# Mixer products in float32r of split weights, with projections in groups of 512 columns

## The chip, the cores and the metric

The kernel runs on one core of one Trainium2 chip. The metric is device time in microseconds (us) of one launch. Inputs, outputs and the reference's arithmetic are float32.

## The reference, cut to what matters

The network has two layers, a sequence of 256 positions and a width of 1024. Each layer first mixes tokens, then runs a mixture of experts (16 experts of width 256). The token mixer is where the change lies:

```
h = modulate(rms_norm(x, g_mix[l]), sh1, sc1)
proj = h @ w_in                      # 256x1024 by 1024x2340
cu, cg, dq, dk, dv, iq, ik, iw, mq, mk, mv = jnp.split(proj, offs, axis=-1)
y_conv = conformer_conv(cu, cg, ...) # gate, 31 taps per channel, layer norm, silu
y_dsa  = dsa_attention(dq, dk, dv, iq, ik, iw)   # 6 heads, each query keeps its top 64 keys
y_moba = moba_attention(mq, mk, mv)  # 6 heads, causal
x = x + g1 * (concatenate([y_conv, y_dsa, y_moba]) @ w_o)   # 256x1024 by 1024x1024
```

Which keys a query keeps depends on iq, ik and iw. The modulation vectors (sh1, sc1, g1, ...) are products of the condition vector with w_ada.

## The kernel before, in words

Everything is kept with features on the partitions: 1024 features are 8 tiles (index k) of 128 partitions by 256 positions. All weights stream from HBM through a ring of 14 buffers of 1 MB each (`pump`, line 72); a buffer is given back by `done` once the work that reads it has been written, and the next load is issued by SyncE into the buffer that comes free.

`mixers` (line 401) does one layer's token mixer. hT is the modulated input (line 408). The projections follow in the order ix (indexer columns and values, 292 columns), cu, cg (`proj_T`, output features on partitions), d0, d1, q0, q1, m0, m1 (`proj`, 256 columns each, output positions on partitions). Each is a float32 product that sums over the 8 k tiles. Between them stand, in the order in which TensorE is to run them: transposes of queries and keys (`flip2`, `transposes`), scores, parts of the modulation products ("ada" parts, line 275, taken from `early`), and the three pairs of indexed attention (`dsa[0]` to `dsa[2]`), each a `score`, a softmax on VectorE and ScalarE, a `flip` (transposes of the probabilities) and a `value` product. Then come `out_part` for the eight k tiles of the output projection (line 646), mixed with the three pairs of causal attention (`blk`).

VectorE has four kinds of work here: `select_keys` (lines 493 to 502; eight rounds of MAX8 and MATCH_REPLACE8 that find the 64 best keys), rotations of queries and keys (`rope_in_place`, lines 461 to 464), the softmax's mask and normalisation (lines 520 to 530), and the convolution's taps (lines 673 and 675, 56 operations of 128x256).

TensorE's order is that of the code (`manual_schedule` in `mixers` fixes TensorE alone). VectorE's and ScalarE's order in `mixers` is set by the scheduler when the kernel is built. Every engine then runs its own queue in that order, and an instruction that waits holds up all that stand behind it on its engine.

In `moe` some products are in float32r already: the gathers of rows (line 936) and the combination of the experts (lines 1017 and 1023) multiply a high and a low part.

Of the kernel before, what the change touches and what calls it, by code (L numbers as in the profile page):

```python
# [19 lines left out]
P = 128  # L20
DM = 1024
KT = DM // P
SEQ = 256
NT = SEQ // P
DEPTH = 2
HD = 64
# [19 lines left out]
IXW = 292  # L46


IN_PARTS = {"cu": 0, "cg": 256, "d0": 512, "d1": 768, "q0": 1188, "q1": 1444, "m0": 1700, "m1": 1956}


@with_exitstack
def block_kernel(ctx: ExitStack, tc: tile.TileContext, x, c, w_ada, b_ada, g_mix, w_in, w_dw, b_dw, ln_conv_g,
                 ln_conv_b, w_o, g_ffn, w_router, b_router, w_gate, w_up, w_down, g_final, rope, out):
    nc = tc.nc
    V, S, G, T = nc.vector, nc.scalar, nc.gpsimd, nc.tensor
# [24 lines left out]
    def done(*keys):  # L81
        for key in keys:
            del wt[key]
            freed[0] += 1
        pump()
# [8 lines left out]
    def add_win(l, *names):  # L94
        for name in names:
            if name == "ix":
                for kh in range(2):
                    rows = w_in[l, kh * 512:(kh + 1) * 512, :].rearrange("(k p) n -> p k n", p=P)
                    loads.append((("win", l, "ix", kh), [P, 4, IXW],
                                  lambda t, r=rows: [(t[:, :, 0:164], r[:, :, 1024:1188]),  # L100
                                                     (t[:, :, 164:IXW], r[:, :, 2212:2340])]))
            else:
                src = w_in[l, :, IN_PARTS[name]:IN_PARTS[name] + 256].rearrange("(k p) n -> p k n", p=P)
                loads.append((("win", l, name), [P, KT, 256], lambda t, src=src: [(t, src)]))

    def add_wo(l):
        for kp in (1, 2, 3, 0):
# [23 lines left out]
    add_ada(0, "sc1", "sh1")  # L131
    for l in range(DEPTH):
        if l == 0:
            add_win(l, "ix", "cu", "cg", "d0", "d1", "q0", "q1")
            add_ada(l, "g1", "sh2")
        else:
            add_win(l, "ix")
            add_ada(l, "g1", parts=(0,))
            add_win(l, "cu")
            add_ada(l, "g1", parts=(1, 2))  # L140
            add_win(l, "cg")
            add_ada(l, "g1", parts=(3,))
            add_win(l, "d0", "d1", "q0", "q1")
            add_ada(l, "sh2")
        add_win(l, "m0", "m1")
# [47 lines left out]
    start = ctx.enter_context(ExitStack())  # L193
# [204 lines left out]
        norm.add(k)  # L398


    def mixers(big, wk, l, norm, early):
        a1, sh1 = mod["sc1", l], mod["sh1", l]
        rs = norm.rs
        hT = big.tile([P, KT, SEQ], F32, name="hT", tag="H")
# [4 lines left out]
        QK = big.tile([P, 10, SEQ], F32, name="QK")  # L409
        VV = big.tile([P, NT, 7 * HD], F32, name="VV")  # L410

        def w_rows(name, k):
            if name == "ix":
                return wt["win", l, "ix", k // 4][:, k % 4:k % 4 + 2, :]
            return wt["win", l, name][:, k:k + 2, :]

        def proj(name, w=256):
            if w <= 256:
                pp = bank([P, NT, w])
                pts = [pp[:, t, :] for t in range(NT)]  # L420
            else:
                pts = [bank([P, w]) for _ in range(NT)]
                pp = pts
            for kh in range(4):
                W = w_rows(name, 2 * kh)
                for kk in range(2):
                    k = 2 * kh + kk
                    for t in range(NT):
                        tt = slice(t * P, (t + 1) * P)
                        first = k == 0 and (w > 256 or t == 0)  # L430
                        last = k == KT - 1 and (w > 256 or t == NT - 1)
                        T.matmul(pts[t], hT[:, k, tt], W[:, kk, :], start=first, stop=last)  # L432
                if name == "ix" and kh % 2 == 1:
                    done(("win", l, "ix", kh // 2))
            if name != "ix":
                done(("win", l, name))
            return pp

        def proj_T(name):
            pp = bank([P, 2, SEQ])  # L440
            for kh in range(4):
                W = w_rows(name, 2 * kh)
                for kk in range(2):
                    k = 2 * kh + kk
                    for cc in range(2):
                        cs = slice(cc * P, (cc + 1) * P)
                        T.matmul(pp[:, cc, :], W[:, kk, cs], hT[:, k, :], start=(k == 0 and cc == 0),  # L447
                                 stop=(k == KT - 1 and cc == 1))
            done(("win", l, name))
            return pp  # L450

# [53 lines left out]
        class Pair:  # L505
# [50 lines left out]
        def heads(name, nrope, tail=None):  # L556
            pp = proj(name)
            pb = t2k([P, NT, 256], "pb")
            if tail is None:
                S.copy(pb, pp)  # L560
            else:
                S.copy(pb[:, :, 0:64 * nrope], pp[:, :, 0:64 * nrope])
                S.copy(tail, pp[:, :, 64 * nrope:256])
            rope_in_place(pb, 0, nrope, HD, 8, 0)
            return pb

        def flip2(dst, pb):
            transposes(dst, [pb[:, :, 0:128], pb[:, :, 128:256]])


        pp = proj("ix", IXW)
# [7 lines left out]
                      pi[:, :, None, 128:160].to_broadcast([P, NT, 4, 32]))  # L579
        iw = sm.tile([P, NT, 4], F32, name="iw", tag="iw")  # L580
        V.tensor_scalar(iw, pi[:, :, 160:164], 0.5, None, OP.mult)


        pu = proj_T("cu")
# [15 lines left out]
        dsa = [Pair(QK[:, i, :], QK[:, 3, :], vd, vd, sel, 2 + i) for i in range(3)]  # L600
# [6 lines left out]
        p0 = heads("d0", 4)  # L607
        p1 = heads("d1", 3, VV[:, :, 0:HD])
# [6 lines left out]
        early.take(8 if l == 0 else 5)  # L615
        flip2(QK[:, 6:8, :], p2)
# [6 lines left out]
        yT = big.tile([P, KT, SEQ], F32, name="yT", tag="H")  # L623
        S.copy(VV[:, :, HD:HD + 256], pp)
        dsa[0].value()
        flip2(QK[:, 4:6, :], p4)
        dsa[1].flip()
# [11 lines left out]
        pos = [bank([P, 2, SEQ]) for _ in range(KT // 2)]  # L639
        nk = [0]  # L640

        def out_part(k):
            ki = nk[0]
            W = wt["wo", l, k // 2][:, k % 2, :]
# [65 lines left out]
        S.activation(yT[:, 0:2, :], yc, AF.Copy, scale=0.5)  # L710
        out_part(4)
        blk[1].value()
        blk[2].flip()
# [601 lines left out]
```

## Time and profile before

| what | us |
|---|---|
| median of 3 runs | 592.7 (591.97 to 592.88) |
| the profiled execution | 593.65 |
| its span, first to last instruction | 591.9 |
| TensorE busy in the span | 549.9 (93%) |
| VectorE busy | 278.5 (47%) |
| ScalarE busy | 158.6 (27%) |
| DMA, mean rate over the span | 309 GB/s |

A float32 product is two MATMUL records in the trace (48 products of `proj` are 96 records), a float32r product is one. Records overlap, since each is shown until its last result lands, so the pace of products is read from the starts of rows and not from the duration of one. A row of the timeline merges equal instructions that follow each other; "x96" is their number. The mark [3.97 <-DVE slb] is the idle time before an instruction and what ended it.

### The profile page before, as it was taken

Reading aid. Unit: us, or ns where it says so; the run is one execution under the profiler, and the core shown is the slowest. Engines: PE = TensorE matmul, PEld = TensorE weight load, DVE = VectorE, ACT = ScalarE, POOL = GpSimd, SP = SyncE. Lnnn points to the kernel's source line nnn. Section 1 sums busy time; section 2 is a strip of 40 time slices with the busy share of each in tenths; the row PEclk is TensorE's granted clock in tenths of the full one; section 3 lists DMA queues with packets and bytes.
Section 4 is the critical chain, followed back from the end, with each engine's and each line's share of the span. In section 5 each row is a group of like instructions: output and inputs, shape, how many; then the busy total and the mean of one; then the engine's idle time right before and its main releaser. Section 6 shows DMA issues by size and latency. Waiting matters only on the chain. (4 is left out here: it accounts for less than half of the span.)

```text
span 591.9 us, 10356 instructions
## 1 busy us (share of the span) xinstructions
PE 549.9 (93%) x3881; PEld 334.9 (57%) x3881; DVE 278.5 (47%) x882; ACT 158.6 (27%) x368; POOL 46.0 (8%) x51
## 2 busy tenths in 40 slices
PE   2799999999979999999969999999997999999993
PEld 0268886677725444444336788667874554444331
DVE  1231999574264333323234099957427533333222
ACT  1141202446242211111144020344624211111113
POOL 1000004000030000000000000500003011111110
PEclk9999999999989999999979999999998999999997
DMA  8999989983499999999999997957349599999932
GB/s 316 384 310 382 399 300 373 405 285 102 141 323 363 363 363 354 360 356 361 393 369 370 385 383 291 352 170 263 117 138 345 177 362 363 362 362 362 356 118 75
DMA packets 126025, 182.82 MB, mean 309 GB/s; under 512 B 7920, under 2 KB 94216, under 8 KB 125960
## 3 DMA queue, kind: packets, MB, share of 16 engines
q1 hardware_dynamic: 125344, 180.80, 88.3%
q10 hardware_dynamic: 616, 1.19, 0.6%
q8 instruction: 36, 0.59, 0.4%
q14 instruction: 29, 0.24, 0.1%
HBM read 180.92 MB, written 1.05 MB: 307 GB/s over the span
## 5 line engine op out<-in xcount | busy, mean ns | idle before, releaser
L958 PE MATMUL bank<-w,XT 128*32 128x512 f32 (+1 forms) x1024 | 112.9, 592 | 0.0
L432 PE MATMUL bank<-w,hT 128*128 128x256 f32 (+1 forms) x448 | 100.9, 385 | 1.1 <-ACT hT L408 1.1
L432 PEld LDWEIGHTS bank<-w,hT 128*128 128x128 f32 x448 | 84.3, 190 | 16.3 <-ACT hT L408 2.1
L958 PEld LDWEIGHTS bank<-w,XT 128*32 128x32 f32 x1024 | 33.5, 110 | 75.1 <-issue 68.7
L996 PE MATMUL bank<-w,eaT 128*32 128x512 f32 (+1 forms) x512 | 58.2, 595 | 0.4
L646 PE MATMUL bank<-yT,w 128*128 128x256 f32 x256 | 57.5, 381 | 0.0
L275 PE MATMUL bank<-w,cB 128*32 128x512 f32 x384 | 53.3, 673 | 3.7 <-DMA w<-in_w_ada 1.8
L646 PEld LDWEIGHTS bank<-yT,w 128*128 128x128 f32 x256 | 48.0, 190 | 6.9 <-issue 0.7
L675 DVE SCALAR_TENSOR_TENSOR cvy<-cva,hw,cvy 128x256 f32<-128x256 f32 x108 | 49.8, 511 | 0.6
L946 DVE SCALAR_TENSOR_TENSOR eac<-eth,bank 128x256 f32<-128x256 f32 x16 | 6.7, 422 | 83.4 <-ACT eth L945 83.4
L936 PE MATMUL bank<-D,gH 128*128 128x256 f32 x128 | 33.2, 297 | 2.4 <-DVE eac L946 2.4
L996 PEld LDWEIGHTS bank<-w,eaT 128*32 128x32 f32 x512 | 15.2, 109 | 32.0 <-issue 28.9
L945 ACT ACTIVATE eth<-bank 128x256 f32<-128x256 f32 x16 | 6.2, 384 | 96.2 <-PE bank L958 96.2
L936 PE MATMUL bank<-D,gL 128*128 128x256 f32 x128 | 31.6, 285 | 0.0
L940 ACT ACTIVATE XT<-bank,sh,sc 128x256 f32<-128x256 f32 x36 | 18.2, 561 | 44.6 <-PE bank L936 44.6
L936 PEld LDWEIGHTS bank<-D,gH 128*128 128x128 f32 x128 | 25.0, 195 | 7.0 <-issue 5.0
L447 PE MATMUL bank<-hT,w 128*128 128x256 f32 x128 | 28.3, 379 | 0.0
L447 PEld LDWEIGHTS bank<-hT,w 128*128 128x128 f32 x128 | 24.2, 190 | 3.3
L984 POOL TENSOR_TENSOR Yl<-yf,Yh 128x512 fp32r<-128x512 f32 x14 | 17.9, 1282 | 95.0 <-ACT Yh L983 95.0
L523 ACT ACTIVATE pr<-pr,nm 128x128 f32<-128x128 f32 (+1 forms) x48 | 21.3, 444 | 14.1 <-DVE nm L520 14.1
L936 PEld LDWEIGHTS bank<-D,gL 128*128 128x128 f32 x128 | 25.0, 195 | 0.0
L275 PEld LDWEIGHTS bank<-w,cB 128*32 128x32 f32 x384 | 10.6, 115 | 25.3 <-issue 17.1
(270 smaller groups left out, 664.0 us busy)
## 6 DMA issues: line engine op xcount, KB each, us to landing
w<-in_w_ada SPq DMA_DIRECT2D x48, 1024.0 KB, 11.8
w<-in_w_gate SPq DMA_DIRECT2D x128, 256.0 KB, 6.0
w<-in_w_up SPq DMA_DIRECT2D x128, 256.0 KB, 6.0
w<-in_w_down SPq DMA_DIRECT2D x64, 512.0 KB, 7.6
w<-in_w_in SPq DMA_DIRECT2D x16, 1024.0 KB, 13.0
w<-in_w_o SPq DMA_DIRECT2D x8, 1024.0 KB, 9.2
w<-in_w_in SPq DMA_DIRECT2D x4, 328.0 KB, 15.5
xin<-in_x ACTq DMA_DIRECT2D x1, 1024.0 KB, 9.9
```

The source lines that it names most:

```text
L275: T.matmul(self.pa[j:j + 32, :], cB[:, 2 * kq + kk, o:o + 32], W[:, kk, h * 512:(h + 1) * 512], start=(u == 0 and kq == 0), stop=(u + 1 == ...
L432: T.matmul(pts[t], hT[:, k, tt], W[:, kk, :], start=first, stop=last)
L447: T.matmul(pp[:, cc, :], W[:, kk, cs], hT[:, k, :], start=(k == 0 and cc == 0), stop=(k == KT - 1 and cc == 1))
L523: S.activation(pr[:, lo:hi], pr[:, lo:hi], AF.Exp, bias=nm[:, u:u + 1], scale=-1.0, accum_out=sums[:, u:u + 1])
L646: T.matmul(pos[n // 2][:, n % 2, :], W[:, n * P:(n + 1) * P], yT[:, k, :], start=(ki == 0 and n % 2 == 0), stop=(ki == KT - 1 and n % 2 == 1))
L675: tap = V.scalar_tensor_tensor(out=cy[:, cc, :], in0=src, scalar=w, in1=cy[:, cc, :], op0=OP.mult, op1=OP.add)
L936: T.matmul(pg[:, i, :], z[:, t, ks], D[:, t, :], start=(si == 0), stop=(si == 3))
L940: S.activation(XT[:, k, :], pg[:, i, :], AF.Identity, bias=sh2[:, k:k + 1], scale=a2[:, k:k + 1])
L946: V.scalar_tensor_tensor(out=ac, in0=th, scalar=1.0, in1=pgu[:, 0, :], op0=OP.add, op1=OP.mult)
L958: T.matmul(pf[b0:b0 + BLK, :], XT[:, k, o + b0:o + b0 + BLK], W[:, e, k % 2, :], start=(k == 0), stop=(k == KT - 1))
L984: (V if whole else G).tensor_tensor(Yl[:, sl], yf, Yh[:, sl].bitcast(F32), OP.subtract)
L996: T.matmul(pd[b0:b0 + BLK, :], aT[:, f, b0:b0 + BLK], W[:, e, f, :], start=(f == 0), stop=(f == 1))
```

## The change

It does five things. hT is split into two float32r tiles: hH is hT rounded by a ScalarE copy, hL is hT minus hH, by VectorE. Every weight tile but ix's is split in the same way by `split`, 512 columns at a time, into WH (ScalarE) and WL (VectorE); four buffers of each exist per name. Every product of cu, cg, d, q, m and of the output projection becomes three float32r products into the same PSUM bank: high by high, low by high and high by low. The projections d0/d1, q0/q1 and m0/m1 become d, q and m of 512 columns, loaded as two halves of four k tiles. The mixers' output yT becomes yH and yL, the low part by VectorE. With d, q and m whole, some of TensorE's steps stand elsewhere: the first indexed pair's scores now stand before m, and all flips of q and the second pair's scores stand behind it. ix, the attention and the experts are as they were.

```diff
+    def split(wk, w, shape):
+        WH = wk.tile(shape, F32R, name="WH", tag="WH", bufs=4)
+        WL = wk.tile(shape, F32R, name="WL", tag="WL", bufs=4)
+        S.copy(WH, w)
+        V.tensor_tensor(WL, w, WH.bitcast(F32), OP.subtract)
+        return WH, WL
...
+        for k in range(0, KT, 2):
+            S.copy(hH[:, k:k + 2, :], hT[:, k:k + 2, :])
+            V.tensor_tensor(hL[:, k:k + 2, :], hT[:, k:k + 2, :], hH[:, k:k + 2, :].bitcast(F32), OP.subtract)
...
+        def proj(name, w):
+            pts = [bank([P, w]) for _ in range(NT)]
+            for k in range(KT):
+                W = wt["win", l, name, k // 4][:, k % 4, :]
+                if name != "ix":
+                    WH, WL = split(wk, W, [P, w])
+                for t in range(NT):
...
+                        T.matmul(pts[t], hH[:, k, tt], WH, start=first, stop=False)
+                        T.matmul(pts[t], hL[:, k, tt], WH, start=False, stop=False)
+                        T.matmul(pts[t], hH[:, k, tt], WL, start=False, stop=last)
...
-                S.copy(yT[:, dst, :], po)
+                S.copy(yH[:, dst, :], po)
+                V.tensor_tensor(yL[:, dst, :], po, yH[:, dst, :].bitcast(F32), OP.subtract)
...
-        p2 = heads("q0", 4)
+        pts = proj("q", 512)
         flip2(QK[:, 0:2, :], p0)
-        p3 = heads("q1", 4)
         transposes(QK[:, 2:4, :], [p1[:, :, 0:128], kd])
+        p2 = heads(pts, 0, 4)
+        p3 = heads(pts, 256, 4)
         early.take(8 if l == 0 else 5)
+        dsa[0].score()
+        pts = proj("m", 512)
...
         flip2(QK[:, 6:8, :], p2)
-        dsa[0].score()
-        p4 = heads("m0", 4)
         flip2(QK[:, 8:10, :], p3)
         dsa[1].score()
         dsa[0].flip()
-        pp = proj("m1")
...
             for n in range(KT):
-                T.matmul(pos[n // 2][:, n % 2, :], W[:, n * P:(n + 1) * P], yT[:, k, :],
-                         start=(ki == 0 and n % 2 == 0), stop=(ki == KT - 1 and n % 2 == 1))
+                if n % 4 == 0:
+                    WH, WL = split(wk, wt["wo", l, k // 2][:, k % 2, n * P:(n + 4) * P], [P, 512])
+                ns = slice((n % 4) * P, (n % 4 + 1) * P)
+                po = pos[n // 2][:, n % 2, :]
+                T.matmul(po, WH[:, ns], yH[:, k, :], start=(ki == 0 and n % 2 == 0), stop=False)
+                T.matmul(po, WH[:, ns], yL[:, k, :], start=False, stop=False)
+                T.matmul(po, WL[:, ns], yH[:, k, :], start=False, stop=(ki == KT - 1 and n % 2 == 1))
```

VectorE's queue in layer 0 around the end of the key selection, before: isc is the selection's score tile, pb the copied queries and keys of d0, cvy the convolution's sum.

```order
L499 MATCH_REPLACE isc<-m_468,isc 128x256
L461 TENSOR_TENSOR ropa<-pb,ropet 128x64
L501 TENSOR_SCALAR isc<-isc 128x384
L462 TENSOR_TENSOR ropb<-pb,ropet 128x4x8
L463 TENSOR_TENSOR ropb<-pb,ropet 128x4x8
L502 TENSOR_TENSOR isc<-isc,causal 128x384
```

The same place in the changed kernel, from the gate's product (cva) on, which stands in front of the selection; w_152 is the first half of d's weights, w_154 its second half, w_187 the first half of q's.

```order
L410 TENSOR_TENSOR WL<-w_152,WH 128x512 x4
L606 SCALAR_TENSOR_TENSOR cva<-sg,bank_405 128x2x256
L502 SCALAR_TENSOR_TENSOR isc<-rl,iw,causal 128x128
...
L508 MATCH_REPLACE isc<-m_574,isc 128x256
L410 TENSOR_TENSOR WL<-w_154,WH 128x512
L510 TENSOR_SCALAR isc<-isc 128x384
...
L410 TENSOR_TENSOR WL<-w_187,WH 128x512
```

The low parts of d's first four k tiles stand in front of the whole selection, that of the fifth behind its last round.

VectorE's queue in layer 0 around the first indexed pair's softmax, before: cvy is the convolution's sum, bank31_702 the pair's scores, pr_710 its probabilities, bank28_641 and bank34_756 transposed queries.

```order
L471 COPY QK_352<-bank28_641 128x512
...
L675 SCALAR_TENSOR_TENSOR cvy_966<-cva_505,hw_967,cvy_966 128x256 x12
...
L520 ISA pr_710,nm_708<-bank31_702,isc_439 128x128
...
L526 RECIPROCAL sums_709<-sums_709 128x4
L530 TENSOR_SCALAR pr_710<-pr_710,sums_709 128x128
...
L471 COPY QK_352<-bank34_756 128x512
```

The same place in the changed kernel: w24_470 and w25_543 are the two halves of m's weights, bank30_903 holds the pair's scores, pr_911 its probabilities.

```order
L410 TENSOR_TENSOR WL_959<-w24_470,WH_958 128x512
L473 TENSOR_TENSOR pb_828<-ropa_831,ropb_832 128x4x16
...
L693 SCALAR_TENSOR_TENSOR cvy_1227<-cva_611,hw_1228,cvy_1227 128x256 x12
L529 ISA pr_911,nm_909<-bank30_903,isc_545 128x128
...
L535 RECIPROCAL sums_910<-sums_910 128x4
L693 SCALAR_TENSOR_TENSOR cvy_1227<-cva_611,hw_1228,cvy_1227 128x256
L539 TENSOR_SCALAR pr_911<-pr_911,sums_910 128x128
...
L410 TENSOR_TENSOR WL_971<-w25_543,WH_970 128x512
```

The low part of m's fifth k tile (WL_971) stands behind twelve taps and that softmax; before, m0 and m1 waited for nothing on VectorE.

## Rows read from the trace of the kernel before

**Rows 1.** Windows view: the two mixer stretches, and the first expert stretch.
```profile
core 0: us, PE busy (x) PEld busy (x) DVE busy (x) ACT busy (x) POOL busy (x), PEclk, DMA share, GB/s
36.00:164.00 128.00, 127.86 (x750) 98.97 (x751) 78.23 (x286) 39.93 (x107) 7.32 (x6) 1.00 0.83 302
316.00:444.00 128.00, 128.00 (x749) 99.00 (x748) 77.35 (x285) 40.16 (x108) 7.54 (x6) 1.00 0.77 270
...
164.00:302.00 138.00, 128.84 (x1124) 61.37 (x1124) 51.58 (x125) 30.21 (x56) 5.19 (x4) 0.97 1.07 360
```

**Rows 2.** Timeline, TensorE, layer 0: start us, us, engine, line, op, operands, records.
```profile
59.20 20.99 PE L432 MATMUL bank<-w,hT 128*128 128x256 f32 x96
80.02 0.60 PE L470 MATMUL bank<-ident,pb 128*128 128x128 f32 x4
...
87.90 7.07 PE L275 MATMUL bank<-w,cB 128*32 128x512 f32 x64
...
105.45 7.07 PE L432 MATMUL bank<-w,hT 128*128 128x256 f32 x32
...
115.36 2.78 PE L275 MATMUL bank<-w,cB 128*32 128x512 f32 x24
...
146.05 14.08 PE L646 MATMUL bank<-yT,w 128*128 128x256 f32 x64
```

**Rows 3.** Timeline, TensorE: float32r products of 256 columns, then of 512.
```profile
179.04 0.28 PE L936 MATMUL bank<-D,gH 128*128 128x256 f32 x1
...
181.99 0.28 PE L936 MATMUL bank<-D,gL 128*128 128x256 f32 x1
...
483.89 0.40 PE L1017 MATMUL bank<-Yh,DT 128*128 128x512 f32 x1
...
485.04 0.39 PE L1017 MATMUL bank<-Yl,DT 128*128 128x512 f32 x1
```

**Rows 4.** Timeline, VectorE, layer 0: selection, taps, a softmax, whole-tile operations.
```profile
59.07 0.69 DVE L596 SCALAR_TENSOR_TENSOR cva<-sg,bank 128x512 f32<-128x512 f32 x1 [6.85 <-ACT sg L593]
59.81 0.75 DVE L493 SCALAR_TENSOR_TENSOR isc<-rl,iw,causal 128x128 f32<-128x128 f32 x2
...
71.84 0.21 DVE L461 TENSOR_TENSOR ropa<-pb,ropet 128x64 f32<-128x64 f32 x1
...
84.70 6.03 DVE L675 SCALAR_TENSOR_TENSOR cvy<-cva,hw,cvy 128x256 f32<-128x256 f32 x15
...
92.53 7.43 DVE L675 SCALAR_TENSOR_TENSOR cvy<-cva,hw,cvy 128x256 f32<-128x256 f32 x12
...
100.48 0.28 DVE L520 CUSTOM_DVE_ANT_0 pr<-bank,isc 128x128 f32<-128x128 f32 x1
...
102.91 1.01 DVE L530 TENSOR_SCALAR pr<-pr,sums 128x128 f32<-128x128 f32 x4
...
141.58 0.69 DVE L703 TENSOR_TENSOR yc<-yc,rsd 128x512 f32<-128x512 f32 x1
142.19 0.55 DVE L543 COPY pT<-bank 128x384 f32<-128x384 f32 x1
```

**Rows 5.** Timeline, ScalarE: table load, gate, and two casts to float32r.
```profile
44.67 1.28 ACT L593 ACT_TABLE_LOAD   x1
58.44 0.60 ACT L593 ACTIVATE sg<-bank 128x512 f32<-128x512 f32 x1 [12.49 <-PE bank L447]
...
169.42 1.14 ACT L800 CAST gH<-xs 128x512 fp32r<-128x512 f32 x2
```

**Rows 6.** Timeline, weight loads of TensorE: one of those products.
```profile
181.87 0.19 PEld L936 LDWEIGHTS bank<-D,gL 128*128 128x128 f32 x1
```

**Rows 7.** Timeline, TensorE, layer 0: an idle of 4 us and what follows.
```profile
173.91 0.17 PE L804 MATMUL bank<-slb,tri 128*128 128x16 bf16 x1 [3.97 <-DVE slb L788]
...
174.13 3.64 PE L275 MATMUL bank<-w,cB 128*32 128x512 f32 x16
...
178.93 0.28 PE L936 MATMUL bank<-D,gL 128*128 128x256 f32 x1
```

More of the change, by code (lines that the diff above doesn't have):

```diff
@@ L101, in add_win @@
                                                      (t[:, :, 164:IXW], r[:, :, 2212:2340])]))
-            else:
+            elif name in ("cu", "cg"):
                 src = w_in[l, :, IN_PARTS[name]:IN_PARTS[name] + 256].rearrange("(k p) n -> p k n", p=P)
                 loads.append((("win", l, name), [P, KT, 256], lambda t, src=src: [(t, src)]))
+            else:
+                for kh in range(2):
+                    src = w_in[l, kh * 512:(kh + 1) * 512, IN_PARTS[name]:IN_PARTS[name] + 512]
+                    src = src.rearrange("(k p) n -> p k n", p=P)
+                    loads.append((("win", l, name, kh), [P, 4, 512], lambda t, src=src: [(t, src)]))
     def add_wo(l):
@@ L142, in block_kernel @@
             add_ada(l, "g1", parts=(3,))
[L143 removed]
+            add_win(l, "d", "q")
             add_ada(l, "sh2")
[L145 removed]
+        add_win(l, "m")
         add_ada(l, "sc2")
@@ L403, in mixers @@
         rs = norm.rs
-        hT = big.tile([P, KT, SEQ], F32, name="hT", tag="H")
+        hT = big.tile([P, KT, SEQ], F32, name="hT", tag="Q")
+        hH = big.tile([P, KT, SEQ], F32R, name="hH", tag="H")
+        hL = big.tile([P, KT, SEQ], F32R, name="hL", tag="L")
         for k in range(KT):
@@ L417, in proj @@
[L417 to L437, printed above, removed]
+        def proj(name, w):
[5 more added lines that the diff above has]
+                for t in range(NT):
+                    tt = slice(t * P, (t + 1) * P)
+                    first, last = k == 0, k == KT - 1
+                    if name == "ix":
+                        T.matmul(pts[t], hT[:, k, tt], W, start=first, stop=last)
+                    else:
+                        T.matmul(pts[t], hH[:, k, tt], WH, start=first, stop=False)
+                        T.matmul(pts[t], hL[:, k, tt], WH, start=False, stop=False)
+                        T.matmul(pts[t], hH[:, k, tt], WL, start=False, stop=last)
+                if k % 4 == 3:
+                    done(("win", l, name, k // 4))
+            return pts
@@ L441, in proj_T @@
             for kh in range(4):
-                W = w_rows(name, 2 * kh)
+                WH, WL = split(wk, wt["win", l, name][:, 2 * kh:2 * kh + 2, :], [P, 2, 256])
                 for kk in range(2):
@@ L446, in proj_T @@
                         cs = slice(cc * P, (cc + 1) * P)
-                        T.matmul(pp[:, cc, :], W[:, kk, cs], hT[:, k, :], start=(k == 0 and cc == 0),
-                                 stop=(k == KT - 1 and cc == 1))
+                        T.matmul(pp[:, cc, :], WH[:, kk, cs], hH[:, k, :], start=(k == 0 and cc == 0), stop=False)
+                        T.matmul(pp[:, cc, :], WH[:, kk, cs], hL[:, k, :], start=False, stop=False)
+                        T.matmul(pp[:, cc, :], WL[:, kk, cs], hH[:, k, :], start=False, stop=(k == KT - 1 and cc == 1))
             done(("win", l, name))
@@ L553, in value, with heads @@
                              stop=True)
-                S.copy(yT[:, dst, :], po)
-        def heads(name, nrope, tail=None):
-            pp = proj(name)
+                S.copy(yH[:, dst, :], po)
+                V.tensor_tensor(yL[:, dst, :], po, yH[:, dst, :].bitcast(F32), OP.subtract)
+        def heads(pts, o, nrope, tail=None):
             pb = t2k([P, NT, 256], "pb")
[L559 to L563, printed above, removed]
+            for t in range(NT):
+                S.copy(pb[:, t, 0:64 * nrope], pts[t][:, o:o + 64 * nrope])
+                if tail is not None:
+                    S.copy(tail[:, t, :], pts[t][:, o + 64 * nrope:o + 256])
             rope_in_place(pb, 0, nrope, HD, 8, 0)
@@ L581, in mixers @@
         V.tensor_scalar(iw, pi[:, :, 160:164], 0.5, None, OP.mult)
+        QK = big.tile([P, 10, SEQ], F32, name="QK", tag="Q")
         pu = proj_T("cu")
@@ L605, in mixers @@
             blk.append(Pair(QK[:, 6 + i, :], QK[:, (9, 4, 5)[i], :], va, vb, causal, 5 + i))
-        p0 = heads("d0", 4)
-        p1 = heads("d1", 3, VV[:, :, 0:HD])
+        pts = proj("d", 512)
+        p0 = heads(pts, 0, 4)
+        p1 = heads(pts, 256, 3, VV[:, :, 0:HD])
         kd = wk.tile([P, NT, P], F32, name="kd", tag="kdup", bufs=1)
         V.tensor_copy(kd.rearrange("p t (r d) -> p t r d", r=2), p1[:, :, None, 128:192].to_broadcast([P, NT, 2, HD]))
-        p2 = heads("q0", 4)
+        pts = proj("q", 512)
         flip2(QK[:, 0:2, :], p0)
-        p3 = heads("q1", 4)
         transposes(QK[:, 2:4, :], [p1[:, :, 0:128], kd])
+        p2 = heads(pts, 0, 4)
+        p3 = heads(pts, 256, 4)
         early.take(8 if l == 0 else 5)
+        dsa[0].score()
+        pts = proj("m", 512)
+        yH = big.tile([P, KT, SEQ], F32R, name="yH", tag="H")
+        yL = big.tile([P, KT, SEQ], F32R, name="yL", tag="L")
         flip2(QK[:, 6:8, :], p2)
-        dsa[0].score()
-        p4 = heads("m0", 4)
         flip2(QK[:, 8:10, :], p3)
@@ L621, in mixers @@
         dsa[0].flip()
-        pp = proj("m1")
-        yT = big.tile([P, KT, SEQ], F32, name="yT", tag="H")
-        S.copy(VV[:, :, HD:HD + 256], pp)
+        p4 = heads(pts, 0, 4)
+        for t in range(NT):
+            S.copy(VV[:, t, HD:HD + 256], pts[t][:, 256:512])
         dsa[0].value()
@@ L709, in mixers @@
         V.scalar_tensor_tensor(out=yc, in0=th, scalar=1.0, in1=yc, op0=OP.add, op1=OP.mult)
-        S.activation(yT[:, 0:2, :], yc, AF.Copy, scale=0.5)
+        S.activation(yH[:, 0:2, :], yc, AF.Copy, scale=0.5)
+        V.scalar_tensor_tensor(out=yL[:, 0:2, :], in0=yc, scalar=0.5, in1=yH[:, 0:2, :].bitcast(F32), op0=OP.mult,
+                               op1=OP.subtract)
         out_part(4)
```

10 lines of the change are left out of this document (2 added, 8 removed).

## The prediction

> **What bounds the kernel now.** I read the windows view first. In both mixer stretches TensorE is busy for the whole 128 us at a granted clock of 1.00, and VectorE has 78 of 128 us of work [rows 1]. So the mixers last as long as TensorE's list of products, and a shorter list pays only while nothing makes TensorE wait. The expert stretch that follows is TensorE's too (128.8 of 138 us), with the DMA share at 1.07; the change leaves it as it is. Next I read TensorE's timeline for the price of a product [rows 2, 3], then the timelines of VectorE and ScalarE for the price of the splits and for what they queue behind [rows 4, 5].
>
> **What the change takes from TensorE.** In a float32 projection, 48 products start within 80.02 − 59.20 = 20.82 us: 0.434 us each; the output projection shows 32 in 14.08, 0.44 each [rows 2]. Float32r products of 256 columns follow each other at (181.99 − 179.04)/25 = 0.118 us, those of 512 at (485.04 − 483.89)/5 = 0.23 (25 and 5 products lie between these starts) [rows 3]. Three in place of one cost 0.354 for 256 columns and 0.69 for 512. Per layer:
> - cu and cg, 32 products: 32 × 0.08 = 2.6 us saved;
> - d, q, m, 48 products of 512 columns in place of 96 of 256: 48 × (0.868 − 0.69) = 8.5 us;
> - the output projection, 64 products: 64 × 0.086 = 5.5 us.
>
> That is 16.6 us a layer and 33.2 in all, if no product waits.
>
> **What it adds to VectorE.** A whole-tile operation of 512 columns has a pace of 142.19 − 141.58 = 0.61 us [rows 4]. A layer gets 52 weight splits, four of hT and some of yT: about 60 × 0.61 = 36 us, so 78 become some 114 of 128. It fits on average; what costs is where a split stands in the queue. The casts (1.14 us for two, 0.57 each [rows 5]) go to ScalarE, which has 40 of 128 us of work [rows 1]; I cost them at nothing except where they stand in a chain below.
>
> **Walk through layer 0.**
>
> *The selection.* d may start 2.6 us earlier, at 59.2 − 2.6 = 56.6. Its first four k tiles are 24 products × 0.23 = 5.5 us: TensorE is through at 62.1. The fifth low part stands behind the whole key selection. That cannot start early: cg ends at 58.4 − 2.6 = 55.8 (its end released the gate [rows 5]); ScalarE then makes the last cast (0.57), loads a table (1.28, which stands behind that cast in its queue now) and runs the gate (0.60), and VectorE makes cva (0.7): 58.9. The selection lasts from 59.81 to 71.84, 12.0 us [rows 4], and the low part 0.6: TensorE goes on at 71.7, after a wait of 9.6 us. Before, d's products ran under the selection without needing VectorE. In layer 1 a modulation part of 1 us stands in that wait: 8.8.
>
> *The clock after the wait.* The trace shows one idle of 4 us: after 3.97 us the records from 173.91 on are at the half level (1.2 GHz), and full pace is back at 178.93 [rows 7]; in that stretch the granted clock is 0.97 over 138 us [rows 1], and nowhere in the mixers does TensorE idle. So 5.0 us at half speed, 2.5 us lost, per layer. Bounds 1.7 and 3.4 (a resume that is two thirds or four thirds as long).
>
> *m.* d ends at 71.7 + 5.5 + 2.5 = 79.7, q's 48 products take 11.0: 90.7, and with the transposes the modulation products start at 91.7 instead of 87.90. They take 7.07 [rows 2], the first pair's scores 0.8, m's first four tiles 5.5: 105.1. The fifth low part stands behind twelve taps and the first softmax. From 71.0 on VectorE has to do before it: 17 splits × 0.61 = 10.4; 37 taps × 0.402 (6.03/15) = 14.9; 32 rotation steps at a pace I take as 0.12 (one shows 0.21, and they overlap) = 3.9; the softmax's four masks and four normalisations, 1.15 + 1.0; copies and the selection's last steps, 2.1; and 2.6 of slow-down, as where 12 taps took 7.43 instead of 4.82 [rows 4]. Sum 36.0: ready at 107.1, a wait of 2.0 us. Layer 1 has one tap fewer in front and a later TensorE; I take 0.7. Bounds 0 and 4.
>
> *Behind m.* m ends at 112.6, which is where m1 ended (105.45 + 7.07 = 112.5 [rows 2]). But the flips of q, the second pair's scores and the first pair's flip, which stood in front of m, now come behind it. The second softmax (mask to last normalisation 100.48 to 103.9, 3.4 us [rows 4]) and the copies of probabilities (0.55 each) lay beside m1's 7 us; now only some 1.4 us of flips and value products lies beside them. Exposed: 3.4 + 0.55 + 0.7 − 1.4 = 3.3 us a layer. Bounds 2.0 (the softmax less the 1.4) and 5.0 (all of it bare).
>
> *The output projection.* It is TensorE's from 120 on, with splits that VectorE makes between taps and softmaxes. I cost small waits at 0.6 a layer, and in layer 1 a further 1.7, where the low part of its first weights stands behind that of yT's last pair: a cast 0.57, that low part some 0.4 and 0.61 in a row, with 0.1 for handing over. Bounds 0 and 4 a layer.
>
> **Sum.** Layer 0: −16.6 + 9.6 + 2.5 + 2.0 + 3.3 + 0.6 = +1.4. Layer 1: −16.6 + 8.8 + 2.5 + 0.7 + 3.3 + 2.3 = +1.0. Loads: the ring's total is unchanged and the mixers use 302 and 270 GB/s against 360 in the experts [rows 1], so I cost the loads in halves at nothing; without that cover each late half would cost TensorE its delay in full. Together +2.4 on the profiled 593.65 gives 596.1. The profiled execution lies 0.95 above the median of 592.7, so on that scale the forecast is 595.1 us.
>
> **Rivals.**
>
> *The splits hide better (faster).* Only the wait at the selection and half of the clock's loss are given back; m's low part is ready, the softmax behind m is covered, the output projection keeps its gain. Then −33.2 + 18.4 + 2.5 + 4.0 for the bare softmax at its lower bound = −8.3: 584.4. For it: every price but the selection's is a balance of two times that differ by little (105.1 against 107.1). Against: the softmax behind m has a known length and little beside it.
>
> *The clock does not come back soon (slower).* After the selection TensorE gets its low parts one by one, and a product of six waits for each. If the bursts leave pauses, the clock may stay at half until q is through: 16.5 us at full speed would take 33 instead of the 19.0 counted above, +14 a layer, 28 in all: 623. It decides if half speed lasts more than some 11 us after the resume. For it: VectorE gives a low part only every 0.61 us or more, with taps between, while six products take 1.38. Against: 0.61 + 0.40 is still less than 1.38, so that bursts run together; and rows 7 show a return within 5 us.
> The Trainium skill's page "TensorE: Matmul & The Clock Gate", section "A second HAM failure mode: psum-queue depth-cycling", speaks for this rival: an engine that idles briefly between groups of products there goes back and forth between half and full clock and loses throughput between bursts. No run here shows that; the one idle of this trace is followed by one return.
>
> *A float32r product is bound by its weights.* Nearly every product of the split form has a stationary tile other than that of the one before, or loads it anew. A load shows 0.19 us [rows 6]; if it set the pace of the 288 products of 256 columns (96 of cu and cg, 192 of the output projection, taken above at 0.118), a layer would cost 288 × 0.07 = 20 more, both 40: 635. Against: the 25 products of rows 3 have a new load each, and still follow at 0.118.
>
> **How the numbers follow.** Chances: the forecast 0.60, the splits hide better 0.25, the clock 0.10, the weights 0.05. The measurement tells 0.2%, some 1.2 us, from no change: faster is under 591.5, slower over 593.9. The forecast's own range, with the bounds of each wait, is 589 to 603; in it I put 0.12 under 591.5, 0.17 between and 0.71 above: 0.07, 0.10 and 0.43 of the whole. The faster rival gives 0.24 to faster and 0.01 to same, the other two 0.15 to slower. So faster 0.31, same 0.11, slower 0.58. The range goes down to 583, which leaves out 0.07 of the faster rival (its waits smaller still), and up to 610, which keeps the clock's milder half (7 us a layer instead of 14) and leaves out 0.05 of it and all of the weights' 0.05.
>
> **What would show it.** In the changed kernel's profile: TensorE idle for 9 to 10 us before d's fifth tile, ended by VectorE's low part, in both layers; a granted clock of half in the 5 us behind it and 1.00 by the end of d; an idle of 0 to 3 us before m's fifth tile; 2 to 5 us of idle between m's end and the last modulation products of that stretch, ended by VectorE's copies; and a w_o stage 4 to 5 us shorter. VectorE should be busy for some 114 of 128 us. The forecast is wrong if the idle before d's fifth tile is under 5 us, if half clock lasts past q, if float32r products of 512 columns run slower than 0.25 us, or if the waits in the output projection come to more than its gain of 5.5.

## The result and the profile after

The changed kernel takes 597.4 us, median of six runs (594.0 to 598.9); the kernel before took 592.6 in the same comparison. The ratio is 1.0075, 95% interval 1.005 to 1.010: slower by 0.75%. The forecast was 595.1, slower, range 583 to 610. The profiled execution took 598.5 us with a span of 596.7.

The windows view of the mixers and of the first experts, with the columns of [rows 1]:

```profile
36.00:164.00 128.00, 115.41 (x762) 90.29 (x766) 111.07 (x344) 68.56 (x165) 5.07 (x6) 0.93 0.81 303
316.00:444.00 128.00, 114.29 (x741) 88.77 (x741) 109.07 (x341) 68.06 (x162) 4.88 (x6) 0.95 0.76 275
164.00:302.00 138.00, 131.88 (x1165) 63.29 (x1157) 51.41 (x126) 30.72 (x58) 5.18 (x4) 0.98 1.04 351
```

Against [rows 1], TensorE (first column after the length) lost 13 us of its 128 to waits and its clock is no longer 1.00; VectorE (third) went from 78 to 111. Where TensorE waits, by the view of waits (total us, times, longest), layer 0 first, then layer 1:

```profile
PE bank L442 <- DVE WL L410: 9.8, 2, 8.9
PE bank L559 <- ACT pT L550: 1.9, 1, 1.9
PE bank L440 <- ACT WH L409: 0.9, 1, 0.9
...
PE bank L442 <- DVE WL L410: 8.3, 1, 8.3
PE bank L665 <- DVE WL L410: 2.9, 1, 2.9
PE bank L559 <- ACT pT L550: 1.8, 1, 1.8
PE bank L547 <- DVE pr L539: 0.3, 1, 0.3
```

L440 to L442 are the three products of d, q and m, L665 is the third of the output projection, L559 the value product. The timeline of TensorE around the first wait (start, us, then the operation):

```profile
58.39 0.50 PE L440 MATMUL bank<-WH,hH 128*128 128x512 f32 x1
...
64.19 0.39 PE L441 MATMUL bank<-WH,hL 128*128 128x512 f32 x1
73.44 0.80 PE L442 MATMUL bank<-WL,hH 128*128 128x512 f32 x1 [8.87 <-DVE WL L410]
74.03 0.63 PE L440 MATMUL bank<-WH,hH 128*128 128x512 f32 x1
...
76.16 0.63 PE L442 MATMUL bank<-WL,hH 128*128 128x512 f32 x1
76.59 0.54 PE L440 MATMUL bank<-WH,hH 128*128 128x512 f32 x1
76.97 0.39 PE L441 MATMUL bank<-WH,hL 128*128 128x512 f32 x1
```

d's fifth tile (64.19) gets its third product at 73.44. Until 76.6 the records last 0.63 and follow each other at 0.43 us, then 0.39 at 0.23: the half clock of the prediction. VectorE in that time, and ScalarE's chain in front of it:

```profile
57.51 0.62 ACT L409 CAST WH<-w 128x512 fp32r<-128x512 f32 x1 [0.82 <-PE bank L456]
58.15 1.28 ACT L603 ACT_TABLE_LOAD   x1
59.44 0.60 ACT L603 ACTIVATE sg<-bank 128x512 f32<-128x512 f32 x1
...
60.08 0.69 DVE L606 SCALAR_TENSOR_TENSOR cva<-sg,bank 128x512 f32<-128x512 f32 x1 [1.22 <-ACT sg L603]
60.68 0.74 DVE L502 SCALAR_TENSOR_TENSOR isc<-rl,iw,causal 128x128 f32<-128x128 f32 x2
...
72.71 0.68 DVE L410 TENSOR_TENSOR WL<-w,WH 128x512 fp32r<-128x512 f32 x1
```

Cast, table, gate, cva, twelve us of selection, and only then the low part. The steps of [rows 2] answer so: the modulation products of 87.90 and 115.36 now start at 91.99 and 122.60. By stage (differences of such starts, after less before):

| stretch | layer 0: measured (predicted) | layer 1: measured (predicted) |
|---|---|---|
| ix to the modulation products behind q | +4.3 (+3.8) | +3.3 (+3.0) |
| from there to those behind m | +3.1 (+2.5) | +0.1 (+1.2) |
| from there to the end of the output projection | −4.3 (−4.9) | +0.4 (−3.2) |

The sum is +6.9 (predicted +2.4). The span grew by 4.8 only: the last expert stretch, from the end of layer 1's output projection on, took 149.0 us here and 151.5 before. Its granted clock (464 to 592 us) was 0.99 here and 0.97 before, some 2.6 us of 128 by estimate. The prediction had nothing there.

### The profile page after: what moved, and what is told of

Same layout as the page of the kernel before. It is cut to its first block, busy times and chain, and to the rows that moved or that the text cites. A ratio compares the mean times of both kernels' runs of the same rounds, so it can differ in the third digit from the quotient of the medians.

```text
span 596.7 us, 10890 instructions
## 1 busy us (share of the span) xinstructions
PE 529.9 (89%) x3977; PEld 321.8 (54%) x3977; DVE 345.3 (58%) x1000; ACT 217.0 (36%) x486; POOL 41.1 (7%) x51
## 5 line engine op out<-in xcount | busy, mean ns | idle before, releaser
L409 ACT CAST WH<-w 128x512 fp32r<-128x512 f32 x96 | 57.8, 621 | 71.4 <-PE bank L441 41.2
L410 DVE TENSOR_TENSOR WL<-w,WH 128x512 fp32r<-128x512 f32 x96 | 63.9, 684 | 17.5 <-ACT WH L409 16.7
L442 PE MATMUL bank<-WL,hH 128*128 128x512 f32 x96 | 39.8, 415 | 18.1 <-DVE WL L410 18.1
L440 PE MATMUL bank<-WH,hH 128*128 128x512 f32 x96 | 39.7, 414 | 0.9 <-ACT WH L409 0.9
L665 PE MATMUL bank<-yH,WL 128*128 128x256 f32 x128 | 37.0, 289 | 2.9 <-DVE WL L410 2.9
L441 PE MATMUL bank<-WH,hL 128*128 128x512 f32 x96 | 38.9, 405 | 0.0
L663 PE MATMUL bank<-yH,WH 128*128 128x256 f32 x128 | 38.0, 297 | 0.0
L664 PE MATMUL bank<-yL,WH 128*128 128x256 f32 x128 | 36.9, 288 | 0.0
L442 PEld LDWEIGHTS bank<-WL,hH 128*128 128x128 f32 x96 | 19.1, 199 | 23.5 <-DVE WL L410 19.4
```

What stands on the lines that cost most here:

```text
L409: S.copy(WH, w)
L410: V.tensor_tensor(WL, w, WH.bitcast(F32), OP.subtract)
L440: T.matmul(pts[t], hH[:, k, tt], WH, start=first, stop=False)
L441: T.matmul(pts[t], hL[:, k, tt], WH, start=False, stop=False)
L442: T.matmul(pts[t], hH[:, k, tt], WL, start=False, stop=last)
L663: T.matmul(po, WH[:, ns], yH[:, k, :], start=(ki == 0 and n % 2 == 0), stop=False)
```

## The experiments

Two theories. A: from the start of the selection to the last tap VectorE has next to no idle time, and that queue sets the pace; a wait taken away comes back elsewhere. What speaks for it is VectorE's share in the changed kernel (third busy column), layer 0:

```profile
60.00:80.00 20.00, 11.13 (x43) 8.82 (x42) 19.93 (x73) 6.33 (x15) 0.00 (x0) 0.74 1.03 401
80.00:100.00 20.00, 20.00 (x131) 12.52 (x130) 20.00 (x62) 9.67 (x23) 5.07 (x6) 1.00 0.64 224
100.00:120.00 20.00, 16.27 (x79) 11.98 (x80) 19.93 (x67) 9.82 (x30) 0.00 (x0) 0.95 1.03 410
120.00:140.00 20.00, 20.00 (x164) 14.52 (x164) 18.84 (x71) 11.43 (x37) 0.00 (x0) 0.97 0.80 270
```

The same stretches before:

```profile
60.00:80.00 20.00, 20.00 (x94) 17.57 (x93) 20.00 (x90) 2.55 (x7) 0.00 (x0) 1.00 1.05 391
80.00:100.00 20.00, 20.00 (x134) 13.00 (x133) 19.75 (x55) 3.21 (x6) 7.32 (x6) 1.00 0.84 313
100.00:120.00 20.00, 20.00 (x134) 13.93 (x133) 11.88 (x55) 8.49 (x30) 0.00 (x0) 1.00 1.02 402
120.00:140.00 20.00, 20.00 (x124) 15.98 (x124) 12.98 (x57) 10.50 (x34) 0.00 (x0) 1.00 0.68 235
```

So a full share by itself does not prove A. From 60 to 100 us VectorE is as full before (20.00 and 19.75), and TensorE never waits, because much of that work is taps, which TensorE needs only at the convolution's mean. What the change adds shows from 100 to 140: 11.88 and 12.98 us have become 19.93 and 18.84. A rival to A is the order of the queue, that is, taps standing in front of low parts and softmaxes. No run moved the taps, so the order and the sum of the work are not told apart.

B, the prediction's own way of reckoning: single waits, each with its price, each to be had back by itself. All ratios below are to the kernel before, run beside each. It took 592.6 us beside the change and 593.2 to 594.8 beside the others, so it is ratios that can be compared, and medians only roughly.

**One wait at a time.** e7 puts the flips of q and the second pair's scores between m's fourth and fifth tile:

```diff
+                if mid and k == 4:
+                    mid()          # flip2 p2, flip2 p3, dsa[1].score()
```

> As changed, but the flips of q and the second pair's scores stand between m's fourth and fifth tile instead of behind m. The second softmax then has four tiles of m (5.5 us) beside it. The waits behind m (1.9, and 1.8 + 0.3 us) should go, and those at m's fifth tile (1.8 and 0) lie under 2 us of flips: 591 to 593. If VectorE's full queue sets the pace there (theory A in its strong form) only part of it: 594 to 596.

Measured 596.8, ratio 1.0035 (1.001 to 1.006): some 2 us gained by the ratios, and the intervals of e7 and the change overlap. The wait behind m came back as two, of 1.5 and 1.4 us, in layer 0.

e8 takes the output projection's first two splits out from behind yL:

```diff
+        wo2 = [split(wk, wt["wo", l, 1][:, 0, n * P:(n + 4) * P], [P, 512]) for n in (0, 4)]
         dsa[2].value()
```

> As changed, but the first two splits of the output projection are written ahead of the third pair's value product, so that in layer 1 the first low part no longer stands behind that of the pair's result. The wait of 2.9 us in layer 1 and the half clock behind it (1.8 us) go: 592.5 to 593.5. If the half clock was not caused by that wait: 594.5.

Measured 596.8, ratio 1.0046 (1.001 to 1.008): against the change the time is inconclusive. Its trace is plain: the wait of 2.9 us in layer 1 is gone, and a few us further on, behind the first part of the output projection, there is this one, for the convolution's last operation:

```profile
PE bank L706 <- DVE cvy L700: 3.2, 1, 3.2
```

Half clock followed that one too, from 416.7 to 420.1.

e6 makes d's eight splits ahead of the selection:

```diff
-RING = 14
+RING = 12                                    # and bufs=8 for WH, WL
+        pre = [split(wk, wt["win", l, "d", k // 4][:, k % 4, :], [P, 512]) for k in range(KT)]
         sel = select_keys(iw)
```

> Eight buffers instead of four for the high and low parts (the weight ring has 12 buffers instead of 14 to make room), and d's eight splits stand in front of the selection in the code and in VectorE's queue. The selection starts 2.4 us later. Theory A: the wait moves from d's fifth tile to q's first, whose low part now stands behind the selection: 75.3 - 69.4 = 5.9 us instead of 8.9 in layer 0; with all of q's and m's splits ahead of the taps the 1.8 us at m go: 3 to 6 us a layer, time 585 to 591. Theory B (only the place of d's fifth low part matters): all of the 8.9 + 1.6 and 8.3 + 2.7 us go: 574 to 577. If the shorter ring starves the experts: over 597.

Measured 601.8, ratio 1.012 (1.008 to 1.016): no gain at all, by the ratios 2.7 us over the change. The wait did move to q's first tile as A said (5.0, in the second line), but the others grew:

```profile
PE bank L559 <- ACT pT L550: 5.0, 1, 5.0
PE bank L442 <- DVE WL L410: 5.0, 1, 5.0
...
PE bank L706 <- DVE cvy L700: 2.3, 1, 2.3
...
PE bank L666 <- DVE WL L410: 4.9, 1, 4.9
```

With the splits ahead, the scheduler put 18 taps (7.2 us) in front of the second softmax; what TensorE no longer waited for at d and m it waited for behind m (5.0), at the convolution's mean (2.3) and, in layer 1, at the output projection (4.9). Here the order of the queue had a part. Theory B's 574 to 577 falls, and so does its way of reckoning e7 (591 to 593); for e8 (592.5 to 593.5) it is the trace that speaks against it, and the time decides little. Theory A named the place where e6's wait would go, but its 585 to 591 was missed by some 10 us. The ring of 12 adds one DMA wait of 1.7 us in the experts.

**VectorE's load itself.** e9 keeps all products and casts but makes no low parts of d, q and m; e10 makes every low part and lets nobody read it. In both the third product reads the input's low part again.

```diff
-                        T.matmul(pts[t], hH[:, k, tt], WL, start=False, stop=last)
+                        T.matmul(pts[t], hL[:, k, tt], WH, start=False, stop=last)
# e9: no WL for d, q, m.   e10: V.tensor_tensor(WL, w, w, OP.subtract), third products of cu, cg, w_o likewise
```

> As changed, with the same list of products and casts, but no low parts of the weights of d, q and m: their third product reads the input's low part and the rounded weights a second time, which costs the same (the weights' low parts are left out of the result). VectorE has 24 x 0.61 = 14.6 us a layer less to do. Theory A (VectorE's full stretch between the selection and the last tap sets the pace, and removing one wait moves it on): the waits at d, m, behind m and at the output projection go nearly all, 14 us in layer 0 and 18 in layer 1; what the steps alone cost (1.75 a layer) stays: 566 to 570. Theory B (the waits are those of single low parts in TensorE's way; those behind m and at w_o are others): only the waits for low parts of d and m and the half clock behind d's go, 8.9 + 1.6 + 1.8 and 8.3 + 2.7: 573 to 575. If the work of TensorE and not VectorE's were the bound: 590 or more.

> As changed, with VectorE making every low part of the weights, but from the weights alone and read by nobody; the third products read the input's low part and the rounded weights a second time. TensorE waits for no low part and VectorE has all the work of the changed kernel, of which some 14 low parts now run ahead of the selection and so some 8 us lie before its full stretch. Theory A: TensorE still waits for VectorE's copies and softmaxes; about 8 us a layer gained, as layer 0 of the first such run showed: 578 to 583. Theory B: 571 to 576, as with the low parts not made.

Measured: e10 582.6, ratio 0.984 (0.979 to 0.990); e9 574.9, ratio 0.968 (0.964 to 0.971). So of the 22 us between the change and e9, some 14 come when no product waits for a low part (and in layer 0 the scheduler sets 14 of d's, q's and m's ahead of the selection), and 8 more by the medians, 10 by the ratios, when VectorE does not make those of d, q and m. The 8 are rough: e10's four runs spread over 6.5 us, and in e9 the low parts of cu, cg and w_o are still read. In e10 no product waits for a low part, and yet TensorE waits for VectorE's and ScalarE's later work, in layer 0 and then in layer 1:

```profile
PE bank L559 <- ACT pT L550: 3.2, 1, 3.2
PE bank L440 <- ACT WH L409: 1.7, 1, 1.7
...
PE bank L705 <- DVE cvy L699: 1.2, 1, 1.2
...
PE bank L705 <- DVE cvy L699: 3.8, 1, 3.8
PE bank L559 <- ACT pT L550: 3.0, 1, 3.0
PE bank L440 <- ACT WH L409: 1.4, 1, 1.4
```

That is theory A, whose 578 to 583 held 582.6 where B had 571 to 576: work that TensorE doesn't read costs it some 8 us. But e9 missed A's 566 to 570 and fell within B's 573 to 575. With VectorE relieved, waits for ScalarE's casts remain (3.2 us in layer 0 and 1.6 in layer 1; the second of layer 0's two and layer 1's stand behind a softmax's exponentials), and the bare softmax behind m (up to 4.4). Neither theory holds by itself. A first form of e10, e1, read the high part a second time:

> The third product of each triple reads the high part of the weights again, so nothing reads a low part; VectorE still makes every low part (from the weights alone, not from the rounded copy). The output is not the reference's. Theory A (VectorE's queue is the bound from the start of the selection to the second softmax, where it has no idle time in the changed kernel: busy 59.4 to 120): d, q and m run through, but TensorE then stands before the flips of the first two softmaxes until VectorE has done the same 57 us of work; second softmax still near 116 us, time 591 to 597. Theory B (single waits, each with its own price): the waits of 8.9 + 1.8 and 8.3 + 2.9 us and the half clock behind them (1.6 and 2.7) go, 26 us: time near 571 to 576.

It took 819 us: with the doubled outputs its experts take another course, with loads of their own that TensorE waits for (up to 3.7 us each). So only its layer 0 can be read. There the output projection ended at 153.3 instead of 163.0, with VectorE as full (40.0 of 40 us from 60 to 100).

**Another engine.** e5 gives the low parts of d, q and m to GpSimd.

```diff
-        V.tensor_tensor(WL, w, WH.bitcast(F32), OP.subtract)
+        (E or V).tensor_tensor(WL, w, WH.bitcast(F32), OP.subtract)    # E is GpSimd for d, q, m
```

> The low parts of d, q and m (24 a layer) are made by GpSimd, those of cu, cg, w_o and the activations still by VectorE. Nothing of d, q, m then stands behind the selection in a queue. GpSimd's add of 128x256 took 0.73 us in the kernel before, so 1.46 us is the guess for 512 columns, against 1.38 that six products take. Theory A (VectorE's full stretch from the selection to the second softmax sets the pace): 14.6 us a layer leave that stretch, less some slow-down where both work; the waits of 8.9 + 1.8 and 8.3 us and the half clock behind them (1.6 and 2.7) go: 574 to 582. Rival (the low part takes over 2 us on GpSimd, or slows VectorE as much as it relieves it): TensorE waits 0.6 us or more for each of 24 tiles, 15 us a layer: 597 or more.

Measured 600.6, ratio 1.010 (1.006 to 1.014). GpSimd made 48 low parts at 1.34 us each, fast enough: d and q ran through and the modulation products started at 80.0 instead of 92.0. Then TensorE stood for VectorE. The longest wait of layer 0:

```profile
PE bank L489 <- DVE QK L480: 7.8, 1, 7.8
```

The timelines of GpSimd and of VectorE's rotations beside it:

```profile
87.89 5.29 POOL L410 TENSOR_TENSOR WL<-w,WH 128x512 fp32r<-128x512 f32 x4
...
89.54 1.28 DVE L470 TENSOR_TENSOR ropa<-pb,ropet 128x64 f32<-128x64 f32 x1
90.74 1.26 DVE L471 TENSOR_TENSOR ropb<-pb,ropet 128x32 f32<-128x32 f32 x1
91.93 1.30 DVE L472 TENSOR_TENSOR ropb<-pb,ropet 128x32 f32<-128x32 f32 x1
```

A rotation step of 0.18 to 0.22 us took 1.26 to 1.30 while GpSimd subtracted: the rival of the expectation, that VectorE is slowed as much as it is relieved. VectorE was busy for all 40 us from 60 to 100, as in the kernel before, and got less done.

**Parts of the change alone.** e2 makes d in one float32 product of the rounded input, without its low part, e4 keeps the groups of 512 and the moved steps and splits nothing, e3 splits w_o alone in the kernel before.

```diff
# e2
+                    elif name == "d":
+                        T.matmul(pts[t], hH[:, k, tt].bitcast(F32), W, start=first, stop=last)
```

> d in one float32 product per tile (of the rounded input alone, its low part left out), the rest as changed. d costs 16 x (0.868 - 0.69) = 2.8 us a layer more on TensorE; its wait for the selection goes. Theory A: VectorE has 8 low parts less, 4.9 us a layer, before the second softmax, and that is all that is gained: about 587. Theory B: waits of 8.9 and 8.3 and the half clock of 1.6 and 2.7 go, 2.8 a layer comes: about 581.

Measured 592.5, ratio 0.999 (0.996 to 1.001): 5 us better than the change, less than either theory. The wait of 8.9 is gone, but in layer 0 those for m's fifth tile (2.7 and 0.4, the longer one for a cast) and behind m (2.4) make 5.5 us where they were 3.7, and half clock followed the first of them (0.58 from 101 to 104.5).

> The kernel before with d, q, m in groups of 512 columns and the steps where the change puts them, all products float32. VectorE has nothing to split. If the second softmax behind m is bare for its own length (prediction, 3.3 us a layer; 1.9 and 2.1 measured as waits in the changed kernel): 596 to 599. If it was bare in the changed kernel only because VectorE came late (theory A in its strong form): 593 to 594.

Measured 597.0, ratio 1.005 (1.0025 to 1.0075): the steps by themselves cost 3 us, with waits of 1.1 and 0.6 us behind m in each layer, nearly as bare as in the change (1.9 and 2.1). In the trace the stretch from the modulation products behind q to those behind m is 2.4 us longer in each layer than before; the prediction had 3.3 for it.

> The kernel before with only the output projection in float32r of split weights. 64 x 0.086 = 5.5 us a layer less on TensorE, 11 in all; 16 low parts and those of yT are 12 us a layer on VectorE, which has 21 of 44 us of work there. Theories A and B: waits of 0.5 to 2 us a layer, time 583 to 585. If the products of 256 columns don't keep 0.118 us when each has new weights: over 590.

Measured 584.1, ratio 0.983 (0.980 to 0.986), within the expectation, but put together otherwise: there is no wait in the mixers beyond the 0.9 us ahead of ix that the kernel before has too, and the w_o stage is 4.3 us shorter in each layer, not 5.5. The products keep their pace of 0.12 us; the gain was reckoned too high by 1.2.

**Versions that beat both.** e11 adds cu and cg to e3, where VectorE has room ahead of the selection; e12 adds q0 and q1.

```diff
+                WH, WL = split(wk, wt["win", l, name][:, 2 * kh:2 * kh + 2, :], [P, 2, 256])    # e11: proj_T
+                if name in ("q0", "q1"):                                                       # e12: proj
+                    WH, WL = split(wk, W, [P, 2, 256])
```

> The kernel before with the output projection, cu and cg in float32r of split weights, d0 to m1 and all steps as before, and a weight ring of 13 buffers to make room. 16.2 us less on TensorE (5.5 + 2.6 a layer); 12 low parts a layer more than with w_o alone, ahead of the selection, where VectorE had 5.7 of 24 us of work. Both theories: 578 to 581, 5 us under w_o alone. If the ring of 13 starves the experts, or the start of the selection moves: 583 or more.

> As e11 (output projection, cu and cg split), and q0 and q1 as well, still 256 columns each and with the steps as before; d and m stay float32 and cover the selection. 32 x 0.08 = 2.6 us a layer less on TensorE, 8 low parts = 4.9 us a layer more on VectorE. In the run before, VectorE had 1.3 us free of 20 at 80 to 100 and 4.5 at 100 to 120, after the selection. Theory A (VectorE's full stretch from the selection sets the pace once its slack is used up): the first softmax comes some 4 us later, TensorE waits for its flip, and the 2.6 us are given back: 575 to 578. If only splits in TensorE's direct way cost (four of the eight now stand ahead of the selection, the others are due 20 us later): 571 to 572.

e11: 576.5, ratio 0.971 (0.968 to 0.975), the fastest kernel that leaves nothing out. TensorE never waits in its mixers behind the start of ix. The time fell by 16.7 us, as much as the 16.2 of the list, but not all of it in the mixers: in the trace each is 6.6 us shorter (cu and cg 2.1 and not 2.6, w_o 4.3 and not 5.5), and 2.5 us lie in the last expert stretch, as in the changed kernel. e12: 577.8, ratio 0.972 (0.969 to 0.976): nothing gained from q, as theory A said, though its reason, a wait for the first softmax's flip, is not in the trace. VectorE (third busy column) at 80 to 100 us in e11:

```profile
80.00:100.00 20.00, 20.00 (x133) 12.94 (x132) 18.68 (x57) 4.48 (x13) 7.32 (x6) 1.00 0.83 314
```

And in e12:

```profile
80.00:100.00 20.00, 18.96 (x138) 12.29 (x137) 19.96 (x60) 3.95 (x12) 7.89 (x6) 1.00 0.94 360
```

With VectorE full (19.96), TensorE has its first idle microsecond there. In e12 its waits are small (1.0 for a low part and 0.2 in layer 0, 0.6 + 0.7 + 0.3 in layer 1): 2.8 of the 6.5 us that are missing against e11 less 5.2. By the starts of its stages, e12's mixers are 0.1 and 0.4 us longer than e11's, so q's gain is given back within them. It was some 2 us a layer and not 2.6: in layer 0 the stretch of d and q got 0.8 us shorter around a wait of 1.0.

## Why the prediction was right

- *The pace of the products* held: 0.12 us (w_o, e3) and 0.23 (from 77 us on in the timeline above), so the rival "bound by its weights" falls. The gain was reckoned too high all the same: cu and cg gave 2.1 us a layer for 2.6 and w_o 4.3 for 5.5, with no wait in it (layer 0 and e3). Three products take 0.36 us and not 0.354, and the first of each group in w_o takes 0.20 to 0.30. With some 8.3 for d, q and m (an estimate from their starts less the waits) the list is some 29 us shorter, not 33. That w_o's 4.3 lies near the 4.9 forecast is luck: the 0.6 of small waits did not come in layer 0, and the missing gain took their place.
- *The selection* was right in mechanism and nearly in size: 8.9 and 8.3 us for 9.6 and 8.8. The whole chain came 1.7 us later than worked out, mostly (1.3) since ix began at half clock in this execution (below).
- *The clock after it*: half for 3.1 us in layer 0 and, from 357.6 to 363.3, 5.7 in layer 1; 1.6 and 2.8 us lost for 2.5 each. The rival that the clock stays at half through q falls. But half clock also followed the shorter waits behind m in layer 0 (1.9 us of idle, then half from 117.9 to 121) and at w_o in layer 1 (2.9 us, then half from 414.8 to 418.2), which the prediction did not charge. The Trainium skill's page "TensorE: Matmul & The Clock Gate", section "A second HAM failure mode: psum-queue depth-cycling", has an engine that idles between groups of products go back and forth between half and full clock; in these four places the trace agrees, while through the bursts of q it stayed at full, as it did behind m in layer 1 after 1.8 us of idle.
- *m*: 1.8 us for 2.0 in layer 0 and none for 0.7 in layer 1. Only half of the 1.8 was for the low part; the other 0.9 was for the tile's cast, which stood behind the softmax's exponentials on ScalarE and which the prediction cost at nothing.
- *Behind m*: the term of 3.3 us a layer was too large; waits of 1.9 and 2.1 measured, 1.7 in e4.
- *The output projection*, layer 1, is the term that was mis-sized most: 0.6 + 1.7 = 2.3 predicted, and the stage lost 4.7 us against layer 0's: 2.9 of wait, and 1.8 of half clock behind it. That is more than the 4.3 that layer 0 gained, so the stage grew by 0.4. VectorE at that place:

```profile
411.65 1.00 DVE L539 TENSOR_SCALAR pr<-pr,sums 128x128 f32<-128x128 f32 x4
412.57 0.42 DVE L564 TENSOR_TENSOR yL<-bank,yH 128x256 fp32r<-128x256 f32 x1
412.90 0.48 DVE L693 SCALAR_TENSOR_TENSOR cvy<-cva,hw,cvy 128x256 f32<-128x256 f32 x1
413.30 0.69 DVE L410 TENSOR_TENSOR WL<-w,WH 128x512 fp32r<-128x512 f32 x1
...
414.04 0.39 PE L665 MATMUL bank<-yH,WL 128*128 128x256 f32 x1 [2.94 <-DVE WL L410]
```

The low part stands behind yL as foreseen, and also behind a normalisation and a tap: VectorE was late with everything, which a chain of three operations doesn't see.

So sign and time came out right, from a sum of single waits whose places were right. That the time came so near (597.4 for 595.1) is luck in part: the mixers grew by 6.9 us where 2.4 were forecast, and 2.5 came back in the last expert stretch, which the prediction left as it was. The experiments show besides that the sum is not made of independent terms: taking any one wait away (e6, e7, e8) gave little or nothing. In layer 0 of the changed kernel VectorE, at 111 of 128 us, has no idle time from 60.1 to 121.7, so whatever passes one wait meets the queue again further on. That VectorE's work costs time by itself is shown by e10 and e9; whether its sum or its order does is not. The prediction's "114 of 128, it fits on average" held the number and drew too little from it. Of the 15 us between e9 and the full saving of 33, some 4 are the list itself; how the rest divides among ScalarE's casts, the steps and the clock was not separated.

## What to carry to other kernels

When a change shifts work from the engine that is the bound to one at 60%, count the second engine's work from the place where it is fullest, not over the stage: 36 us into 50 free ones would have fitted only if they could run before the selection or after the taps. Take first the parts whose new work falls where the helper is idle (w_o, cu and cg: 16.7 us gained), and stop at the part for which the first engine begins to wait (q: nothing gained). A full share alone is no such sign, as VectorE's before the change shows; what stands in front of the new work in the queue has to be read too. A wait that goes when its cause is removed, and returns further on for another tile of the same engine, points to a full queue; the test is work that nobody reads.

## What the runs showed of the hardware

- VectorE's two-tensor operations stretched beside GpSimd's in e5: 1.28 us for a rotation step, the length of one GpSimd subtraction (1.34), while MAX8 and MATCH_REPLACE8 of 256 columns kept their 0.40 us beside it. Twelve taps in 7.43 us [rows 4], with GpSimd additions of 0.73 to 0.85 us beside them, were perhaps the mild form. The Trainium skill's page "SBUF — State Buffer", section "Who interferes with whom", says that a VectorE instruction with two SBUF inputs and a GpSimd instruction that reads SBUF shut each other out for a whole instruction; the trace agrees. Operations on one tensor were not safe either: the four normalisations (L539) took 4.09 us beside GpSimd's subtractions at 105.4, and 0.99 in the changed kernel.
- The clock fell to half after an idle of 0.92 us ahead of ix in the profiled execution of the changed kernel, and not after one of 0.93 at the same place before. The timeline and the windows view at 36 to 39 us, in the changed kernel:

```profile
35.83 9.82 PE L438 MATMUL bank<-w,hT 128*128 128x292 f32 x32 [0.92 <-ACT hT L422]
36.00:39.00 3.00, 3.00 (x7) 2.11 (x8) 2.83 (x8) 2.94 (x7) 0.00 (x0) 0.50 1.09 362
```

And before:

```profile
36.01 8.13 PE L432 MATMUL bank<-w,hT 128*128 128x292 f32 x32 [0.93 <-ACT hT L408]
36.00:39.00 3.00, 2.99 (x12) 2.38 (x13) 2.65 (x7) 2.56 (x6) 0.00 (x0) 1.00 1.09 363
```

It cost 1.5 us. The changed kernel's runs spread over 4.9 us, those of e11, which has no waits in its mixers, over 0.3; but the kernel before has none either, and its runs spread over 2.4 us beside the change and 4.4 beside e5 to e8. What the spread comes from was not tested.
